# Seven products of a feed-forward tile tied in order on the tensor engine, and the second down weight of a tile made behind the sum that frees its accumulator

## The chip, the core and the metric

The kernel runs on one core of a Trainium2 chip. The metric is the device time of one execution in microseconds (us), the median of several executions. The kernel before takes 1226.12 us (three runs, 1225.51 to 1226.54). Besides these timed runs there is one profiled execution; every duration below comes from it.

The engines are named as in the profile: PE (tensor engine, matmuls), PEld (its weight loads), DVE (vector engine), ACT (scalar engine), POOL and SP (here they issue transfers). Each engine works through its own list of instructions in the order in which the program put them there.

## The reference

One decoder layer on 512 tokens of width 1024: a feed-forward, a mixer (attention and a recurrence, merged), and a second feed-forward. The change touches the two feed-forwards alone:

```python
def swiglu(x, w_gate, w_up, w_down):
    return (jax.nn.silu(x @ w_gate) * (x @ w_up)) @ w_down

f = swiglu(rms_norm(h, ffn1_norm_pre[l]), ffn1_w_gate[l], ffn1_w_up[l], ffn1_w_down[l])
h = h + 0.5 * rms_norm(f, ffn1_norm_post[l])
...
f = swiglu(rms_norm(h, ffn2_norm_pre[l]), ffn2_w_gate[l], ffn2_w_up[l], ffn2_w_down[l])
h = h + 0.5 * rms_norm(f, ffn2_norm_post[l])
```

The hidden width is 2816, that is 22 tiles of 128 columns. All inputs are float32.

## The kernel before, in words

**Numbers.** A float32 operand is split into a high part (a copy on ACT, rounded to the matmul's format) and a low part (source minus high part, on DVE); `split` does both, and its two instructions appear in the profile as L269 (ACT) and L270 (DVE). A product is three matmuls for each piece of the contraction: high by high, high by low, low by high.

**Feed-forward tiles.** `ffn` runs over the hidden tiles f = 0 to 21. The first n0 tiles (6 in the first feed-forward, 4 in the second) are plain. From f = n0 on a tile computes gate and up for all 512 tokens with seven products of half-size blocks in place of eight (a Strassen-Winograd scheme; the halves are of the contraction, of the tokens, and gate against up). `prod` issues them: p1, p5, p6, p2, p7, p3, p4, each twelve matmuls of 256 columns (lines 977 to 979). They accumulate in three places: `b` (bank 0 or 1, by turns from tile to tile) takes p1, p6, p7 and p4; `z` (bank 5) takes p5 and p3; `y` (bank 2) takes p2 on top of a copy of p1. Partial results are copied out on ACT between two products of one accumulator (L985 for c5 and c6, L998 for y), and added to later accumulator values on DVE (`sum_of`, L990). The sum of `b` and c5 after p7 must have read `b` before p4 may write it.

**Weights of a tile.** `w_forms_in_place` adds and splits a tile's weights one tile ahead (`prep`), with a priority that puts them ahead of the tile's own work. In the profile these are the rows w<-raw of L269 and L270, and the sums L623 to L627.

**Down projection.** Four hidden tiles at a time also go through a seven-product scheme. A `window` after a tile holds one to three of its products, run by `step` (matmuls of 512 columns, lines 891 to 893, two times six for each product). The windows are (p1, p2), (p5), (p6, p7), (p3, p4) in turn; in the first feed-forward the first eight tiles' products are caught up after f = 7 to 12, where two windows hold three products: (p1, p2, p5) after f = 7 and after f = 10. The weights of a step are made by `down_form`: a load by POOL into a buffer (`dr` or `npair`), a split into one of two buffers (`wd`, by turns), and then the issue of the load for the next product that uses the same source buffer (`supply`). The first two weights of a window (`due`) are made inside `prod`, between p2 and p7; the third is made inside the window behind its first step. Of all windows 24 have at least two weights and 6 have one.

**Order.** A scheduler puts the instructions of each engine in a list: at each point of its own model of time it takes the ready instruction of highest priority; priority is the order of the program, moved ahead by an offset where `tc.high_priority` says so (`AHEAD` = 100 for weights of the next tile, `EVAC` = 200 for copies and sums out of the accumulators). `tc.issue_after(ins)`, wrapped here as `behind(...)`, adds for each instruction of a block on the engine of `ins` that it comes behind `ins` in that engine's list; instructions of the block on other engines aren't touched. Before the change p1 of a tile is behind the last matmul before it, the steps likewise; the other six products are held by their data alone. In the kernel before, `down_form` for both weights stands in `behind("copy")`, behind the ACT copy c6.

Of the kernel before, what the change touches and what calls it, by code (L numbers as in the profile page):

```python
# [154 lines left out]
def hybrid_layer(ctx: ExitStack, tc: tile.TileContext, xT: bass.AP, xN: bass.AP, wst: bass.AP,  # L155
                 first: bass.AP, rows: bass.AP, wdn: bass.AP, wbig: bass.AP, consts: bass.AP, bias: bass.AP, out: bass.AP):
    nc = tc.nc
    DVE, ACT, PE = nc.vector, nc.scalar, nc.tensor
# [109 lines left out]
    def split(dh, dl, src):  # L268
        ACT.activation(dh, src, AF.Copy)  # L269
        DVE.tensor_sub(dl, src, dh.bitcast(F32))  # L270

    def acc_ps():
        turns["acc"] += 1
        return banks[(turns["acc"] - 1) % turns["n"]]
# [5 lines left out]
    def tmp(name):  # L280
        return tpool.tile([P, T], F32, name=name, tag="t")
# [503 lines left out]
    def ffn(n, x, r, forms_x, home, pss):  # L785
# [53 lines left out]
        def last_act(f):  # L839
            v = home.slot((f - LAST[0] - 1) % 8)  # L840
            return v[:, 0, :], v[:, 1, :]
# [12 lines left out]
        def supply(a, p):  # L854

            if p in ("p5", "p6", "p3"):
                dst, qs = home.x, {"p5": ("u0", "u1"), "p6": ("g0",), "p3": ("g1",)}[p]
            else:
                dst, qs = dr[p in ("p2", "p4")], {"p1": ("g0",), "p2": ("g1",), "p7": ("u0", "g0"), "p4": ("u1",)}[p]
            for i, q in enumerate(qs):  # L860
                load(dst, a, q, i > 0 or p in ("p6", "p3"))
            at[p] = dst
# [3 lines left out]
        def down_form(a, p):  # L866
            w = wdt[home.n % 2]
            home.n += 1
            split(w[:, 0, :], w[:, 1, :], at[p])
            ready[p] = w  # L870
            q = NEXT[p]
            a += p in ("p7", "p3", "p4")
            if a < SEVEN:
                supply(a, q)
# [78 lines left out]
        last = {}  # L953

        @contextmanager
        def behind(*engines):
            with ExitStack() as es:
                for e in engines:
                    if e in last:
                        es.enter_context(tc.issue_after(last[e]))  # L960
                yield

        def prod(f, w, due):

            g = tmp("g")
            b, y, z = b_of[f % 2][:, :HB], y_[:, :HB], z_[:, :HB]
            u = ub[:, f % 4, :] if 4 < f < LAST[0] else tmp("u")
            if n == 1 and f in (6, 8):
                u = tmp("u")

            def product(p, ps, start):
                if len(t[p][0].shape) == 4:
                    ps = ps.rearrange("q (b t) -> q b t", b=2)
                for k in range(4):
                    ks = slice(k * P, (k + 1) * P)
                    wh, wl, xh, xl = w[p][:, 0, ks], w[p][:, 1, ks], t[p][0][:, k], t[p][1][:, k]
                    PE.matmul(ps, wh, xh, start=start and k == 0, stop=False, skip_group_check=True)  # L977
                    PE.matmul(ps, wh, xl, start=False, stop=False, skip_group_check=True)  # L978
                    i = PE.matmul(ps, wl, xh, start=False, stop=k == 3, skip_group_check=True)  # L979
                last["PE"] = i.ins  # L980

            def copy(ps):
                c = tpool.tile([P, HB], F32, name="c", tag="c", bufs=CB)
                with tc.high_priority(offset=EVAC):
                    last["copy"] = ACT.activation(c, ps, AF.Copy).ins  # L985
                return c

            def sum_of(dst, ps, c):
                with tc.high_priority(offset=EVAC):
                    DVE.tensor_add(dst, ps, c)  # L990

            lead = f == n0
            with behind("PE"):
                product("p1", b, True)
            c1 = copy(b) if lead else None
            if not lead:
                with tc.high_priority(offset=EVAC):
                    ACT.activation(y, b, AF.Copy)  # L998
            product("p5", z, True)
            c5 = copy(z)  # L1000
            product("p6", b, False)
            c6 = copy(b)
            product("p2", y, lead)
            if lead:
                sum_of(g[:, lo_], y, c1)
            with behind("copy"):
                for a, p in due:
                    down_form(a, p)
            product("p7", b, False)
            sum_of(u[:, hi_], b, c5)  # L1010
            with tc.high_priority(offset=EVAC):
                ACT.activation(g[:, lo_], g[:, lo_] if lead else y, AF.Silu)
            product("p3", z, False)
            sum_of(g[:, hi_], z, c6)
            product("p4", b, False)
            last["ACT"] = ACT.activation(g[:, hi_], g[:, hi_], AF.Silu).ins
            with tc.high_priority(offset=EVAC):
                DVE.scalar_tensor_tensor(u[:, lo_], g[:, lo_], -1.0, b, op0=ALU.mult, op1=ALU.mult)
            last["DVE"] = DVE.scalar_tensor_tensor(u[:, hi_], g[:, hi_], -1.0, u[:, hi_], op0=ALU.mult,
                                                   op1=ALU.mult).ins  # L1020
            return u
# [41 lines left out]
        for at_, ev in enumerate(order):  # L1063
# [16 lines left out]
            elif ev[0] == "prep":  # L1080
                with behind("DVE", "ACT"):
                    forms[ev[1]] = w_forms_in_place(("gu", n, ev[1]))
            elif ev[0] == "prod":
                due = order[at_ + 1]
                u = prod(ev[1], forms.pop(ev[1]), [(due[1], p) for p in due[2][:2]] if due[0] == "window" else [])
                if ev[1] == 4:
                    part0(u)
            elif ev[0] == "finish":
                finish(ev[1], u)
            else:  # L1090
                for i, p in enumerate(ev[2]):
                    with behind("PE"):
                        step(ev[1], p)
                    if len(ev[2]) > 2 and i == 0:
                        down_form(ev[1], ev[2][2])
        with behind("ACT"):
            warm(eps)
        last = Act(*zip(*(last_act(f) for f in range(*LAST))))
# [295 lines left out]
    with ExitStack() as mx:  # L1394
# [127 lines left out]
        for hd in range(NH):  # L1522
# [9 lines left out]
            for kind, c in FILL[hd]:  # L1532
                if kind == "attn":
                    ws = fetch((kind, c))
                    for i in range(2):
                        ps = acc_ps()
                        gemm(ps, [w[:, i * T:(i + 1) * T] for w in ws], attn)
                        DVE.tensor_mul(facc[:, 2 * c + i, :], ps, facc[:, 2 * c + i, :])
                else:
                    ps = acc_ps()  # L1540
# [10 lines left out]
        for c in range(KC):  # L1551
            ps = acc_ps()
# [155 lines left out]
```

## Time and profile before

| | before |
|---|---|
| median of three runs | 1226.12 us (1225.51 to 1226.54) |
| the profiled execution, its own time | 1225.54 us |
| its span, first to last instruction | 1223.8 us |
| DVE busy | 974.9 us (80%) |
| ACT busy | 737.9 us (60%) |
| mean granted TensorE clock | 0.999 |
| matmuls of 256 columns, start to start when nothing is waited for | 0.12 us |
| the like of 512 columns | 0.23 us |

The profiled execution's time is 1.74 us more than its span, for what lies around the instructions, and 0.58 us below the median. A matmul's row gives a duration longer than the distance to the next one, since matmuls are pipelined; the distance between starts is what counts. An idle time in brackets at the end of a row is that of its engine just before, with the work that ended it.

### The profile page before, as it was taken

How to read it: one execution, taken by the hardware profiler on the slowest of the kernel's cores; microseconds unless marked ns; L12 is line 12 of the kernel's file. 1: busy time of each engine (PE TensorE's matmuls, PEld its weight loads, DVE VectorE, ACT ScalarE, POOL GpSimd, SP SyncE). 2: the span in 40 equal slices, each digit the busy share in tenths (PEclk: the TensorE clock that was granted, in tenths of full speed). 3: DMA queues.
4: the chain of work that ended last, by engine and by line, in shares of the span. 5: the costliest groups of instructions: out<-in, count | busy, mean ns of one | idle time of the engine just before them, and what ended most of it. 6: DMA issues, size and time to landing. Idle time of an engine off the chain costs nothing.

```text
span 1223.8 us, 19282 instructions
## 1 busy us (share of the span) xinstructions
PE 1211.8 (99%) x7664; PEld 1097.9 (90%) x7664; DVE 974.9 (80%) x1525; ACT 737.9 (60%) x1234; POOL 82.3 (7%) x135
## 2 busy tenths in 40 slices
PE   9999999999999999999999999999999999999997
PEld 8898989999878899999998888888899999999996
DVE  7998878988579887888766798755788887979864
ACT  7566665655556564656665787724556665656462
POOL 0001111100102000000000000000110010101000
PEclk9999999999999999999999999999999999999999
DMA  6336646464725222222234234324463555555441
GB/s 246 138 104 172 169 113 175 141 166 115 259 105 181 104 81 102 78 79 102 72 140 151 89 121 155 129 99 165 141 190 108 160 156 145 153 142 164 112 155 69
DMA packets 36986, 166.57 MB, mean 136 GB/s; under 512 B 4128, under 2 KB 7328, under 8 KB 24864
## 3 DMA queue, kind: packets, MB, share of 16 engines
q1 hardware_dynamic: 18288, 107.13, 24.8%
q0 software_dynamic: 18608, 58.20, 18.2%
q8 instruction: 60, 0.98, 0.3%
q14 instruction: 30, 0.25, 0.1%
HBM read 153.26 MB, written 7.86 MB: 132 GB/s over the span
## 4 chain that ended last, share of the span: by engine, by line
PE 94%; DVE 3%; ACT 1%; issue 1%; DMA 0%; DVEq 0%; ACTq 0%
PE bank L977 9%; PE bank L978 9%; PE bank L979 9%; PE bank L284 8%; PE bank L285 8%; PE bank L286 8%; PE bank L644 5%; PE bank L645 5%; PE bank L646 5%; PE bank L892 4%; PE bank L891 4%; PE bank L893 4%; PE bank L397 3%; PE bank L398 3%; PE bank L399 3%; DVE w L270 1%
## 5 line engine op out<-in xcount | busy, mean ns | idle before, releaser
L270 DVE TENSOR_TENSOR w<-raw,w 128x1024 fp32r<-128x1024 f32 (+1 forms) x272 | 297.5, 1103 | 68.4 <-ACT w L269 62.8
L269 ACT ACTIVATE w<-raw 128x1024 fp32r<-128x1024 f32 (+1 forms) x272 | 255.8, 960 | 96.3 <-PE bank L286 40.3
L977 PE MATMUL bank<-big,w 128*128 128x256 f32 x816 | 233.8, 287 | 3.0 <-DVE u L990 1.3
L978 PE MATMUL bank<-big,w 128*128 128x256 f32 x816 | 230.7, 283 | 0.0
L979 PE MATMUL bank<-big,w 128*128 128x256 f32 x816 | 229.4, 283 | 0.0
L977 PEld LDWEIGHTS bank<-big,w 128*128 128x128 f32 x816 | 156.2, 191 | 7.9 <-DVE u L990 2.0
L978 PEld LDWEIGHTS bank<-big,w 128*128 128x128 f32 x816 | 156.3, 192 | 1.6
L979 PEld LDWEIGHTS bank<-big,w 128*128 128x128 f32 x816 | 155.7, 192 | 0.0
L891 PE MATMUL bank<-wd,act 128*128 128x512 f32 x224 | 87.8, 392 | 0.0
L892 PE MATMUL bank<-wd,act 128*128 128x512 f32 x224 | 87.7, 392 | 0.0
L893 PE MATMUL bank<-wd,act 128*128 128x512 f32 x224 | 87.2, 389 | 0.0
L284 PE MATMUL bank<-big,w 128*128 128x512 f32 x176 | 68.5, 389 | 0.0
L285 PE MATMUL bank<-big,w 128*128 128x512 f32 x176 | 68.5, 389 | 0.0
L286 PE MATMUL bank<-big,w 128*128 128x512 f32 x176 | 68.5, 389 | 0.0
L644 PE MATMUL bank<-big,w 128*128 128x256 f32 x228 | 66.1, 290 | 0.0
L646 PE MATMUL bank<-big,w 128*128 128x256 f32 x228 | 64.8, 284 | 0.0
L285 PE MATMUL bank<-act,w 128*128 128x512 f32 (+1 forms) x184 | 64.7, 352 | 0.0
L286 PE MATMUL bank<-act,w 128*128 128x512 f32 (+1 forms) x184 | 64.7, 352 | 0.0
L284 PE MATMUL bank<-act,w 128*128 128x512 f32 (+1 forms) x184 | 64.6, 355 | 0.0
L645 PE MATMUL bank<-big,w 128*128 128x256 f32 x228 | 64.5, 283 | 0.0
L985 ACT ACTIVATE c<-bank 128x256 f32<-128x256 f32 x70 | 26.8, 383 | 61.0 <-PE bank L979 60.6
L270 DVE TENSOR_TENSOR wd<-npair,wd 128x1024 fp32r<-128x1024 f32 x24 | 29.4, 1224 | 39.2 <-ACT wd L269 39.2
(393 smaller groups left out, 3148.5 us busy)
## 6 DMA issues: line engine op xcount, KB each, us to landing
raw<-in_w SPq DMA_DIRECT2D x90, 1024.0 KB, 4.8
dr<-in_wdn POOLq DMA_DIRECT2D x40, 512.0 KB, 5.7
npair<-in_wdn POOLq DMA_DIRECT2D x32, 512.0 KB, 5.5
big<-act POOLq DMA_DIRECT2D x6, 512.0 KB, 3.3
h<-in_x SPq DMA_DIRECT2D x8, 256.0 KB, 5.1
h<-in_xn POOLq DMA_DIRECT2D x4, 512.0 KB, 5.2
raw<-in_wbig SPq DMA_DIRECT2D x2, 1024.0 KB, 4.7
kept_m<-h POOLq DMA_DIRECT2D x4, 512.0 KB, 2.9
```

The lines of the kernel that those rows point to most:

```text
L269: ACT.activation(dh, src, AF.Copy)
L270: DVE.tensor_sub(dl, src, dh.bitcast(F32))
L284: PE.matmul(ps, wh, xh, start=first, stop=False)
L285: PE.matmul(ps, wh, xl, start=False, stop=False)
L286: PE.matmul(ps, wl, xh, start=False, stop=last)
L644: PE.matmul(ps, wh, xh, start=start and k == 0, stop=False, skip_group_check=True)
L891: PE.matmul(ps, xh, wh, start=start and k == 0, stop=False, skip_group_check=True)
L892: PE.matmul(ps, xh, wl, start=False, stop=False, skip_group_check=True)
L893: i = PE.matmul(ps, xl, wh, start=False, stop=k == 1, skip_group_check=True)
L977: PE.matmul(ps, wh, xh, start=start and k == 0, stop=False, skip_group_check=True)
L978: PE.matmul(ps, wh, xl, start=False, stop=False, skip_group_check=True)
L979: i = PE.matmul(ps, wl, xh, start=False, stop=k == 3, skip_group_check=True)
```

## The change

Each of the seven products is now put in `behind("PE")`: on PE it comes behind the last matmul traced before it, so that the order is p1, p5, p6, p2, p7, p3, p4, then the steps of the window, then the next tile. The first weight of a window is still made behind the copy c6. The second (`due[1:]`) is traced behind the sum that follows p7, in `behind("sum")`; that sum is a DVE instruction, so that the DVE half of the split comes behind it on DVE. The ACT half of the split and the load that follows are in the block too, but on other engines.

```diff
             def sum_of(dst, ps, c):
                 with tc.high_priority(offset=EVAC):
-                    DVE.tensor_add(dst, ps, c)
+                    last["sum"] = DVE.tensor_add(dst, ps, c).ins
...
-            product("p5", z, True)
+            with behind("PE"):
+                product("p5", z, True)
             c5 = copy(z)
-            product("p6", b, False)
+            with behind("PE"):
+                product("p6", b, False)
             c6 = copy(b)
-            product("p2", y, lead)
+            with behind("PE"):
+                product("p2", y, lead)
             if lead:
                 sum_of(g[:, lo_], y, c1)
             with behind("copy"):
-                for a, p in due:
+                for a, p in due[:1]:
                     down_form(a, p)
-            product("p7", b, False)
+            with behind("PE"):
+                product("p7", b, False)
             sum_of(u[:, hi_], b, c5)
+            with behind("sum"):
+                for a, p in due[1:]:
+                    down_form(a, p)
             with tc.high_priority(offset=EVAC):
                 ACT.activation(g[:, lo_], g[:, lo_] if lead else y, AF.Silu)
-            product("p3", z, False)
+            with behind("PE"):
+                product("p3", z, False)
             sum_of(g[:, hi_], z, c6)
-            product("p4", b, False)
+            with behind("PE"):
+                product("p4", b, False)
```

## The prediction

> **What bounds the kernel now.** I read the page first, then the idle time of the tensor engine (PE) along its timeline, then the vector engine (DVE) and scalar engine (ACT) around each of its waits.
>
> ```profile
> span 1223.8 us, 19282 instructions
> PE 1211.8 (99%) x7664; PEld 1097.9 (90%) x7664; DVE 974.9 (80%) x1525; ACT 737.9 (60%) x1234; POOL 82.3 (7%) x135
> ```
>
> PE is busy for all but 12 us, so the change can win only what the feed-forwards lose in waits, and can lose whatever new waits it makes. The windows below are stages of PE work: the first three hold the places where the order on PE departs from the program's, the last is an undisturbed tile.
>
> ```profile
> 98.03:113.00 14.97, 13.58 (x98) 12.49 (x97) 12.52 (x19) 8.76 (x14) 2.28 (x3) 1.00 0.54 108
> 149.75:164.84 15.09, 14.97 (x108) 13.80 (x107) 9.33 (x13) 9.15 (x15) 1.71 (x2) 1.00 0.44 87
> 164.84:180.11 15.27, 14.75 (x99) 13.31 (x98) 14.38 (x23) 8.98 (x16) 1.10 (x2) 1.00 0.52 143
> 963.08:978.70 15.62, 15.62 (x110) 14.62 (x108) 13.51 (x20) 11.34 (x20) 1.43 (x2) 1.00 0.53 155
> ```
>
> The columns are the stretch, its length, and the busy time of PE, PEld, DVE, ACT and POOL, then the granted clock, DMA share and GB/s. The last stretch is one tile (84 matmuls of 256 columns) and two steps (24 of 512 columns): 15.62 us, PE never idle. With a step of twelve at 0.228 (2.74 us), the contents of the others without a wait would be: the first, one step and a tile, 15.62 - 2.74 = 12.88, so it loses 2.09; the second, the same and 11 products' matmuls of the next tile's p5 at 0.12, 14.20, loses 0.89; the third, two steps and a tile less those 11, 14.30, loses 0.97. Together 3.95 us, most of what the two feed-forwards lose at all, and the ceiling of a gain.
>
> **Tying the products.** It adds no instruction. In nearly all tiles PE already runs p1, p5, p6, p2, p7, p3, p4, so that the tie changes nothing there. The departures follow the two windows with three down products.
>
> ```profile
> 98.03 0.39 PE L891 MATMUL bank<-wd,act 128*128 128x512 f32 x1
> 98.26 0.28 PE L977 MATMUL bank<-big,w 128*128 128x256 f32 x1
> ...
> 100.56 0.38 PE L977 MATMUL bank<-big,w 128*128 128x256 f32 x1 [0.47 <-ACT c L985]
> ...
> 101.26 0.40 PE L892 MATMUL bank<-wd,act 128*128 128x512 f32 x1
> ...
> 96.36 1.05 ACT L269 ACTIVATE wd<-npair 128x1024 fp32r<-128x1024 f32 x1
> ...
> 99.51 1.22 DVE L270 TENSOR_TENSOR wd<-npair,wd 128x1024 fp32r<-128x1024 f32 x1
> ...
> 151.26 1.22 DVE L270 TENSOR_TENSOR wd<-npair,wd 128x1024 fp32r<-128x1024 f32 x1
> ```
>
> The third product's weight is made inside the window. Its first matmul (L891, at 98.03) needs the high part alone; the second (L892) needs the low part, which DVE finishes at 99.51 + 1.22 = 100.73. In between PE does p5 of the next tile and five matmuls of p3. Tied, it has nothing to do there: from 98.26 to 100.78 (a release takes 0.05, by the sum and the matmul of the chain below) it waits 2.52 us. The second such window starts at 149.75, its low part is there at 152.48: from 149.98 to 152.53, 2.55 us. What was late next goes: the wait of p3 for the copy c5 (0.47 idle at 100.56) and its like in the two later stretches, because p6 and p2 again lie between p5 and p3. So the 3.95 us of the three stretches become 5.07: **+1.12 us**. Bounds: DVE could take this split as soon as ACT is done (96.36 + 1.05 = 97.41), since only sums stand before it; then it ends at 98.63 and each wait is some 0.4, a gain; or one more pass of 1.22 comes ahead of it, 3.74 each. I take the times of before, since nothing ahead of these two splits on DVE waits for PE's later order.
>
> The clock in these stretches is granted at 1.00, and the longest distance between two starts there, 110.26 to 111.46, leaves it so. The Trainium skill (TensorE: Matmul & The Clock Gate, Part 1: The HAM clock gate) says that a window of about 3.4 us without work halves PE's clock until it has been busy as long; by it 2.5 us stay free of charge and 3.74 would not, which no run here shows.
>
> **The second down weight.** Per tile with two weights it moves one ACT copy (1.05), one DVE subtraction (1.22) and the loads that follow, 24 times. On DVE the subtraction leaves its place ahead of the sum. In one tile that place costs PE a wait:
>
> ```profile
> 109.85 1.22 DVE wd L270
> 111.07 0.35 DVE u L990
> 111.41 0.04 issue
> 111.46 0.39 PE bank L977
> ```
>
> The chain of waits shows p4 at 111.46 released by the sum, which stood behind the second weight; p3's last matmul was at 110.26, so 1.08 us, already in the 2.09 above. In the others the sum is just in time:
>
> ```profile
> 968.95 1.22 DVE L270 TENSOR_TENSOR wd<-npair,wd 128x1024 fp32r<-128x1024 f32 x1 [1.76 <-ACT wd L269]
> 970.10 1.22 DVE L270 TENSOR_TENSOR wd<-dr,wd 128x1024 fp32r<-128x1024 f32 x1
> 971.23 0.42 DVE L990 TENSOR_TENSOR ub<-bank,c 128x256 f32<-128x256 f32 x1
> ...
> 971.59 0.28 PE L979 MATMUL bank<-big,w 128*128 128x256 f32 x1
> 971.71 0.38 PE L977 MATMUL bank<-big,w 128*128 128x256 f32 x1
> ...
> 964.77 0.37 ACT L998 ACTIVATE bank<-bank 128x256 f32<-128x256 f32 x1 [0.60 <-PE bank L979]
> 966.15 0.39 ACT L985 ACTIVATE c<-bank 128x256 f32<-128x256 f32 x1 [1.01 <-PE bank L979]
> ...
> 968.82 1.05 ACT L269 ACTIVATE wd<-dr 128x1024 fp32r<-128x1024 f32 x1
> ...
> 970.03 2.01 ACT L269 ACTIVATE w<-raw 128x1024 fp32r<-128x1024 f32 x2
> ```
>
> What will DVE do in the freed 1.22? The tie holds DVE alone: ACT's half of the split loses its place behind c6. Its source and its buffer are ready early in the tile, and ACT idles there (0.60 ahead of 964.77, 1.01 ahead of 966.15), so the scheduler will put it there. It can push the copy at 964.77 by at most 0.45, to an end of 965.59, which its reader, two products later, doesn't feel. Then ACT has nothing between the first weight's copy and the copy of the next tile's weights (now at 970.03), and is in the state of a tile with one weight:
>
> ```profile
> 955.74 1.22 DVE L270 TENSOR_TENSOR wd<-npair,wd 128x1024 fp32r<-128x1024 f32 x1 [2.31 <-ACT wd L269]
> 957.18 1.23 DVE L270 TENSOR_TENSOR w<-raw,w 128x1024 fp32r<-128x1024 f32 x1 [0.22 <-ACT w L269]
> 958.32 0.42 DVE L990 TENSOR_TENSOR ub<-bank,c 128x256 f32<-128x256 f32 x1
> ...
> 956.10 1.05 ACT L269 ACTIVATE w<-raw 128x1024 fp32r<-128x1024 f32 x1
> ...
> 958.38 0.28 PE L979 MATMUL bank<-big,w 128*128 128x256 f32 x1
> 958.79 0.38 PE L977 MATMUL bank<-big,w 128*128 128x256 f32 x1
> ```
>
> There the next tile's weight (w<-raw) is ready a moment before p7 is done, DVE starts its 1.23 at 957.18, and the sum ends later than in the tile with two: p4 follows p3 after 0.41 in place of 0.12. That is **0.29 us** a tile. It decides the case: the sum that the change moves forward finds another subtraction in front of it, which starts 0.2 later than the one taken away.
>
> How many tiles: of the 24, six have the second weight behind the sum already. Twelve with f below 16 do not; among them are the two that follow the three-product windows. Six more (f = 17, 19, 20 in both feed-forwards) are like the one-weight tile f = 18:
>
> ```profile
> 126.62 0.42 DVE L990 TENSOR_TENSOR ub<-bank,c 128x256 f32<-128x256 f32 x1
> ...
> 1091.40 0.42 DVE L990 TENSOR_TENSOR ub<-bank,c 128x256 f32<-128x256 f32 x1
> ...
> 269.92 0.28 PE L979 MATMUL bank<-big,w 128*128 128x256 f32 x1
> 270.07 0.39 PE L977 MATMUL bank<-big,w 128*128 128x256 f32 x1
> ```
>
> The first two rows are the sums of the first and the last of ten tiles like the one at 963 (the other two are the following ones of the three-product windows); the last two show f = 18, where p4 loses 270.07 - 269.92 - 0.12 = 0.03. So 12 x 0.29 = 3.48 and 6 x 0.03 = 0.18: **+3.66 us**. Bounds: 0, if DVE takes the sum first, to 18 x 0.29 = 5.2. I take the value of the one-weight tiles, the nearest rows.
>
> Behind the sum the second subtraction falls in the gap before p4's end, as in the six tiles that have it there:
>
> ```profile
> 1049.86 1.22 DVE L270 TENSOR_TENSOR wd<-dr,wd 128x1024 fp32r<-128x1024 f32 x1
> ...
> 1051.86 0.39 PE L892 MATMUL bank<-wd,act 128*128 128x512 f32 x1
> ```
>
> It ends at 1051.08 and its first reader starts at 1051.86: 0.78 to spare, covered by the first step. If one more pass of 1.22 comes between, PE waits 0.44. The load behind it:
>
> ```profile
> dr<-in_wdn POOLq DMA_DIRECT2D x40, 512.0 KB, 5.7
> ```
>
> POOL issues it when the subtraction is through, so some 2 to 3 us later; 5.7 to land still leaves it ready before the next tile's down weights are made behind c6, about 13 us on. Later loads on POOL's queue wait for their own subtractions anyway. I cost it at nothing; a load that ACT reached too early would hold the copies behind it on ACT, below 1 us in the few tiles where the same buffer is needed at once.
>
> **Sum.** 1.12 + 3.66 = +4.78 us. The profiled execution's own time, 1225.54 (1.74 around its span), becomes 1230.3; it lay 0.58 below the median of 1226.12, so the median becomes **1230.9**.
>
> **The rivals.**
>
> *Sum first.* DVE takes the sum as soon as p7 is done, ahead of the next tile's weight; no 0.29 anywhere, and the two long waits remain: +1.12, **1227.2**. For it: in the tiles with two weights DVE is free 0.2 us before the sum is ready and the priority of a sum is higher; against it: all six one-weight tiles have the subtraction first, and it is ready first.
>
> *Faster.* The scheduler, which sees PE idle in the three-product windows, or an ACT relieved by earlier copies, brings their splits to DVE once ACT is done: two waits of 0.4, no other: 0.8 for 3.95, -3.15, **1223.0**. It decides if the splits start before 98.0 and 149.6. Against it: the sums ahead of them are next-tile work with a higher priority.
>
> *Second weight late.* With the next tile's subtractions first, the second weight slips by one more pass: 18 x 0.44 = 7.9 more, **1238.8**. For it: 0.78 is all there is; against it: six tiles hold it.
>
> *Long waits longer.* One more pass of 1.22 in each of the two, 2.4 more: **1233.3**. By the page on the clock gate, half the clock for some 3.4 us would add an estimated 1.7 to each.
>
> *Nothing done.* PE's order is the program's already and the order on DVE settles as before: 1226.1. Against it: the rows between 98.26 and 101.26.
>
> **How the numbers follow.** Forecast 0.47, sum first 0.17, faster 0.16, second weight late 0.12, longer waits 0.04, nothing done 0.04. The likeliest's own range is 1228.5 to 1233.5. The whole range reaches from the faster case to beyond the longer waits: 1222.8 to 1236; the late weight is left out. Faster by over 0.2% (2.45 us, about what a measurement tells from no change): 0.16; within it, sum first and nothing done, 0.21; slower 0.63.
>
> **What would show it.** Right: no L977 row between rows of L891 to L893; PE idle about 2.5 us inside each three-product window, ended by DVE wd L270; in the tiles with two weights DVE's order wd, w, sum, with p4 some 0.4 after p3's last matmul; ACT's copy of the second weight ahead of c6. Wrong: the sum right behind the first wd (then 1227.2); the 2.5 us shorter, or PE waits of L892 in ordinary windows.

## The result, and the profile after

The changed kernel takes 1257.36 us (median of six runs, 1253.26 to 1259.87) against 1226.21 before: a ratio of 1.0248, 95% interval 1.0238 to 1.0259. The forecast was 1230.9, with a range to 1236. The direction was right, the size wrong by 26 us. Of the executions behind the numbers below one, of the kernel without ties and with the subtraction alone moved, took 1472.84 us at a granted clock of 0.753; it enters no ratio.

From the page of the kernel after, its span, the busy times, the chain of waits by engine, and the median landing time of one kind of load; its profiled execution took 1259.35 us:

```profile
span 1257.6 us, 19277 instructions
PE 1226.1 (98%) x7664; PEld 1107.7 (88%) x7664; DVE 977.2 (78%) x1525; ACT 742.0 (59%) x1234; POOL 82.4 (7%) x135
...
PE 83%; DVE 7%; DMA 4%; issue 3%; ACT 2%; POOL 1%; DVEq 0%; ACTq 0%; POOLq 0%
...
dr<-in_wdn POOLq DMA_DIRECT2D x40, 512.0 KB, 6.7
```

The span grew by 33.8 us (1257.6 - 1223.8). Two things are to be seen. PE has the same 7664 matmuls, but is busy for 14.3 us more: the same work ran slower somewhere. And the chain now runs through transfers (DMA 4%) and POOL; the load dr<-in_wdn lands in 6.7 us, 5.7 before. The view of waits (engine and line, what it waited for, total us, times, longest) names the place. Before, and then after:

```profile
PE bank L977 <- ACT bank L998: 0.3, 1, 0.3
```

```profile
PE bank L977 <- ACT bank L998: 17.8, 7, 3.9
...
ACT wd L269 <- DMA dr<-in_wdn: 22.8, 6, 5.0
```

L998 is ACT's copy of p1 from `b` to `y`, and p6, which overwrites `b`, can't start before it has read `b`. PE's wait for it grew by 17.5 us. The second row says why ACT is late: six times its copy of a down weight waits for that weight's load. Before there is no such row. The timeline of one of the six places, after, sorted by engine (start, duration, engine, line, in brackets the idle time before and what ended it):

```profile
1003.41 1.23 DVE L270 TENSOR_TENSOR wd<-npair,wd 128x1024 fp32r<-128x1024 f32 x1 [1.69 <-ACT wd L269]
1006.00 0.42 DVE L990 TENSOR_TENSOR ub<-bank,c 128x256 f32<-128x256 f32 x1
1007.80 1.22 DVE L270 TENSOR_TENSOR wd<-dr,wd 128x1024 fp32r<-128x1024 f32 x1
...
1005.00 0.54 POOL L850 DMA_DIRECT2D npair<-in_wdn  x1 [10.94 <-DVE wd L270]
1009.21 0.87 POOL L848 DMA_DIRECT2D npair<-in_wdn  x1 [3.67 <-DMA npair<-in_wdn]
1009.78 0.84 POOL L850 DMA_DIRECT2D dr<-in_wdn  x1
...
1017.64 1.06 ACT L269 ACTIVATE wd<-dr 128x1024 fp32r<-128x1024 f32 x1 [3.08 <-DMA dr<-in_wdn]
1018.60 0.37 ACT L998 ACTIVATE bank<-bank 128x256 f32<-128x256 f32 x1
...
1016.22 0.28 PE L979 MATMUL bank<-big,w 128*128 128x256 f32 x1
1019.02 0.39 PE L977 MATMUL bank<-tx,w 128*128 128x256 f32 x1 [2.52 <-ACT bank L998]
```

The same tile and the next one before the change, likewise:

```profile
985.71 1.22 DVE L270 TENSOR_TENSOR wd<-dr,wd 128x1024 fp32r<-128x1024 f32 x1
986.85 0.42 DVE L990 TENSOR_TENSOR ub<-bank,c 128x256 f32<-128x256 f32 x1
...
987.29 0.54 POOL L850 DMA_DIRECT2D dr<-in_wdn  x1 [0.53 <-DVE ub L990]
990.28 0.88 POOL L848 DMA_DIRECT2D npair<-in_wdn  x1 [2.45 <-DMA npair<-in_wdn]
...
996.01 0.37 ACT L998 ACTIVATE bank<-bank 128x256 f32<-128x256 f32 x1 [0.60 <-PE bank L979]
998.83 0.38 ACT L985 ACTIVATE c<-bank 128x256 f32<-128x256 f32 x1 [1.06 <-PE bank L979]
999.11 2.00 ACT L269 ACTIVATE wd<-dr 128x1024 fp32r<-128x1024 f32 x2
```

This is a window of p3 and p4; p4's split frees the buffer `dr`, and its load fetches the weight of p2 for the very next window. Two ends moved towards each other:

- The load starts later. Measured from the start of the tile's sum (L990), POOL issued it after 0.44 us before (987.29 - 986.85) and after 3.78 now (1009.78 - 1006.00). Nearly all of that is the subtraction, which stood ahead of the sum and now ends at 1009.02. POOL adds its own part: its list has the two loads of p5's weight ahead, and the second, which adds onto the first, waits 3.67 us for the first to land; p2's load goes out 0.76 us after its buffer is free (1009.78 - 1009.02).
- It is wanted sooner. Before, ACT's copy stood behind c6 and came to its turn at 999.11, 11.8 us after the issue. Now it stands in ACT's list ahead of L998; ACT reaches it at 1014.56 (1017.64 - 3.08), 4.8 us after the issue. The load needs 7.8.

ACT executes its list in order, so L998 waits with the weight, and p6 behind L998. The other five places are the tiles whose second weight is p2's as well; start to start, less 0.12 for the matmul, the six waits are 2.4, 2.9, 3.8, 2.7, 4.1 and 2.6 us.

The second part of the loss stands in the windows of time (stretch, its length, busy time of PE, PEld, DVE, ACT and POOL, granted clock, DMA share, GB/s). After:

```profile
99.12:102.53 3.41, 1.55 (x6) 0.96 (x6) 3.39 (x5) 0.41 (x1) 0.52 (x1) 1.00 0.97 246
102.53:105.95 3.42, 3.42 (x11) 2.73 (x10) 2.65 (x5) 1.00 (x2) 0.35 (x1) 0.50 0.73 139
...
1078.74:1082.16 3.42, 1.60 (x14) 1.40 (x12) 1.96 (x4) 0.00 (x0) 0.00 (x0) 1.00 0.78 231
1082.16:1085.57 3.41, 1.31 (x11) 1.31 (x12) 0.00 (x0) 1.63 (x3) 0.00 (x0) 1.00 0.00 1
1085.57:1088.98 3.41, 3.41 (x19) 3.41 (x18) 1.23 (x1) 1.55 (x3) 0.00 (x0) 0.50 0.00 0
...
1013.89:1017.30 3.41, 2.61 (x22) 2.40 (x21) 1.51 (x3) 0.67 (x2) 0.00 (x0) 1.00 0.68 213
1017.30:1020.72 3.42, 1.70 (x14) 1.70 (x15) 0.00 (x0) 1.63 (x3) 0.00 (x0) 1.00 0.02 5
...
1150.42:1153.83 3.41, 3.41 (x18) 3.41 (x17) 0.96 (x1) 1.33 (x2) 0.00 (x0) 0.50 0.00 0
```

In seven stretches of 3.41 us, the first at 102.53 and the last at 1150.42, PE's granted clock is 0.50. Six of them lie behind five of the six waits, the first behind a three-product window. They hold 23.2 us of PE work, which would take half of that at full clock: by this estimate 11.6 us are lost. So the span's 33.8 are 17.5 of waits for L998, 11.6 of half clock, and 4.7 of all else. That this is near the 4.78 that the forecast held for the whole is not a test of its terms; they are looked at below.

### The profile page after: what moved, and what is told of

It reads as the page before. It is cut to its first block, busy times and chain, and to the rows that moved or that the text cites. A ratio compares the mean times of both kernels' runs of the same rounds, so it can differ in the third digit from the quotient of the medians.

```text
span 1257.6 us, 19277 instructions
## 1 busy us (share of the span) xinstructions
PE 1226.1 (98%) x7664; PEld 1107.7 (88%) x7664; DVE 977.2 (78%) x1525; ACT 742.0 (59%) x1234; POOL 82.4 (7%) x135
## 4 chain that ended last, share of the span: by engine, by line
PE 83%; DVE 7%; DMA 4%; issue 3%; ACT 2%; POOL 1%; DVEq 0%; ACTq 0%; POOLq 0%
PE bank L284 8%; PE bank L285 8%; PE bank L286 8%; PE bank L977 7%; PE bank L978 7%; PE bank L979 7%; PE bank L644 5%; PE bank L645 5%; PE bank L646 5%; DMA dr<-in_wdn 4%; PE bank L398 3%; PE bank L399 3%; PE bank L397 3%; PE bank L892 3%; PE bank L893 3%
## 5 line engine op out<-in xcount | busy, mean ns | idle before, releaser
L977 PE MATMUL bank<-big,w 128*128 128x256 f32 x816 | 236.4, 290 | 2.3 <-DVE u L990 0.4
L978 PE MATMUL bank<-big,w 128*128 128x256 f32 x816 | 233.6, 286 | 0.0
L979 PE MATMUL bank<-big,w 128*128 128x256 f32 x816 | 233.2, 286 | 0.0
L977 PEld LDWEIGHTS bank<-big,w 128*128 128x128 f32 x816 | 159.3, 195 | 7.6 <-DVE ub L990 4.7
L978 PEld LDWEIGHTS bank<-big,w 128*128 128x128 f32 x816 | 159.0, 195 | 1.3
L979 PEld LDWEIGHTS bank<-big,w 128*128 128x128 f32 x816 | 158.9, 195 | 0.0
L892 PE MATMUL bank<-wd,act 128*128 128x512 f32 x224 | 88.4, 395 | 1.8 <-DVE wd L270 1.8
L893 PE MATMUL bank<-wd,act 128*128 128x512 f32 x224 | 88.0, 393 | 0.0
L270 DVE TENSOR_TENSOR wd<-dr,wd 128x1024 fp32r<-128x1024 f32 x32 | 39.0, 1219 | 39.3 <-ACT wd L269 39.3
L644 PE MATMUL bank<-big,w 128*128 128x256 f32 x228 | 66.0, 290 | 0.0
L646 PE MATMUL bank<-big,w 128*128 128x256 f32 x228 | 64.7, 284 | 0.0
L645 PE MATMUL bank<-big,w 128*128 128x256 f32 x228 | 64.5, 283 | 0.0
```

The source lines that it names most:

```text
L892: PE.matmul(ps, xh, wl, start=False, stop=False, skip_group_check=True)
```

## The experiments

**The two parts apart.** First the ties alone, with both weights left behind c6; then the second weight alone, without ties:

```diff
-            product("p5", z, True)
+            with behind("PE"):
+                product("p5", z, True)
...
             with behind("copy"):
                 for a, p in due:
                     down_form(a, p)
```

> The seven products tied as in the change; both down weights behind the copy c6 as before. Theory (the scalar engine runs into a load that is not there): the six waits of 2.4 to 4.1 us are not there, since the scalar copy of the second weight keeps its place; the two three-product windows cost about 3.4 us of waits and 1.7 of half clock for the 3.95 they lost before, so 1227 to 1229 us, six waits of p6 absent. Rival (the ties leave the tensor engine without work to fill its waits): most of the 31 us is here, 1245 or more.

```diff
             product("p5", z, True)
...
             with behind("copy"):
-                for a, p in due:
+                for a, p in due[:1]:
                     down_form(a, p)
...
             sum_of(u[:, hi_], b, c5)
+            with behind("sum"):
+                for a, p in due[1:]:
+                    down_form(a, p)
```

> The second weight behind the sum as in the change; no ties. Theory: the six waits stay, because p5 and p3 can't fill them (the copy c5 is held on the scalar engine too), so 1248 to 1256 us with a lower granted clock. Rival (ties): about 1226 us.

The ties alone take 1227.56 us, ratio 1.0008 (0.9998 to 1.0018): no difference that can be told. The second weight alone takes 1258.03, ratio 1.0256 (1.024 to 1.0271), 2 us over the range expected. The whole loss is in the second part, and the ties neither make nor mend it. The waits of the second kernel show the same pair of rows as the full change:

```profile
PE bank L977 <- ACT bank L998: 21.0, 8, 4.5
...
ACT wd L269 <- DMA dr<-in_wdn: 25.1, 6, 5.5
```

**ACT's copy put back behind c6** in the changed kernel, the DVE half left behind the sum; once for all second weights, once for those of p2 alone:

```diff
             sum_of(u[:, hi_], b, c5)
-            with behind("sum"):
+            with behind("copy", "sum"):
                 for a, p in due[1:]:
```

> The change, with the scalar half of the second weight kept behind the copy c6 as before (behind copy and sum). Theory: no scalar copy waits for a load ahead of the copies that free the accumulators, the sum stands behind one subtraction: 1225 to 1229 us, clock 1.00. Rival (the move on the vector engine or the ties): 1240 or more.

```diff
             sum_of(u[:, hi_], b, c5)
-            with behind("sum"):
-                for a, p in due[1:]:
+            for a, p in due[1:]:
+                with behind("sum", *(["copy"] if p == "p2" else [])):
                     down_form(a, p)
```

> The change, with the scalar half kept behind c6 for p2's weight alone (the six tiles whose load comes from the window just before); the other second weights may go early as in the change. Theory: 1257.4 - 18.4 (six waits) - about 9 (half clock behind them) = 1230 us, the 0.3 us waits of p4 stay in the other tiles. Rival (all early copies cost alike): 18 of 24 tiles keep their cost, about 1250 us.

They take 1229.29 us, ratio 1.0021 (1.0011 to 1.003), and 1231.88 us, ratio 1.0043 (1.0028 to 1.0057); the first is 0.3 us over its range. One more tie on ACT, in the tiles where p2's weight is the second, takes back 25 of the 31 us (1257.36 - 1231.88 = 25.5). In the other tiles the early copy costs 2.6 us more (1231.88 - 1229.29): p4 loses 3.4 us there by the sum's later place on DVE, and nothing where all copies are kept. The second of these kernels is the change without its one fault, and lies 1.0 us from the forecast.

**No load to wait for.** The two kernels above move ACT's copy. They do not show whether that copy harms by its own 1.05 us, or by the load in front of it. So the copy stays early and the load goes:

```diff
             for i, q in enumerate(qs):
-                load(dst, a, q, i > 0 or p in ("p6", "p3"))
+                if p != "p2" or a == 0:
+                    load(dst, a, q, i > 0 or p in ("p6", "p3"))
             at[p] = dst
```

> The changed kernel, without the loads that p4's split issues for p2 (the first p2 keeps its load; the later ones split what lies in the buffer, so this part of the down weights is left out of the result). The instructions on PE, DVE and ACT and their order stay. Theory (ACT's early copy of p2's weight waits for a load that lands late, and holds the copies y and c that PE needs): the six waits of 2.4 to 4.1 us, 18.4 together, and the half clock behind them, some 8.8, go: 1230, between 1227 and 1233. Rival (the early copy delays ACT by its own 1.05 and DVE's new order does the rest, whatever the load does): the six waits stay, over 1250. Rival (the load is only half of it): 1236 to 1246.

1231.59 us, ratio 1.0035 (1.0022 to 1.0049). The longest waits of PE in the feed-forwards are now those of the three-product windows (one line is added, so that L892 is L893 here):

```profile
PE bank L893 <- DVE wd L270: 1.8, 2, 1.2
```

The row of waits for the copy of p1 is gone, and so is every stretch at half clock in the feed-forwards. The instructions on PE, DVE and ACT come in the same order in this trace as in that of the changed kernel. So the copy's early place by itself makes PE wait for no copy of p1; the load is what ACT, and behind it PE, waited for. The rival in which the six waits come of the copy's own 1.05 us falls.

**POOL's part of the lateness.** The load for p2 is issued by SP, so that it no longer stands behind the two loads of p5:

```diff
             else:
-                nc.gpsimd.dma_start(dst, stored(a, q))
+                (nc.sync if q == "g1" and dst is dr[1] else nc.gpsimd).dma_start(dst, stored(a, q))
```

> The changed kernel with the load for p2 issued by SP in place of POOL, so that it doesn't stand behind the two loads of p5 (the second of which waits for the first to land). Theory (the load is late above all since the subtraction that frees its buffer now follows the sum; POOL's list holds it some 0.8 us more): each of the six waits shortens by about 0.8, 5 in all, and perhaps a half-clock stretch or two go: 1248 to 1253. Rival (its place on POOL's list, and the transfers beside it, make the lateness): the waits fall under 1 us, 1230 to 1238. Rival (neither: SP's own list holds it as long): 1256 to 1260.

1248.14 us, ratio 1.0176 (1.0161 to 1.0191): 9 us back of the 31, not 25. From its waits and its list of transfers:

```profile
PE bank L977 <- ACT bank L998: 6.6, 2, 3.4
...
ACT wd L269 <- DMA dr<-in_wdn: 22.2, 7, 4.0
...
dr<-in_wdn SPq DMA_DIRECT2D x8, 512.0 KB, 8.3
```

Four of the six waits fell to 1.6 us or less, two stayed over 3. But ACT still waits 22.2 us for the load (22.8 in the changed kernel): the load is as late as it was. The four waits fell because the scheduler also changed ACT's order, among the six tiles in just those four. There the copy of p1, L998, now stands ahead of the weight's copy, and only c5 stands behind it:

```profile
195.16 0.37 ACT L998 ACTIVATE bank<-bank 128x256 f32<-128x256 f32 x1 [1.09 <-PE bank L979]
198.16 1.06 ACT L269 ACTIVATE wd<-dr 128x1024 fp32r<-128x1024 f32 x1 [2.63 <-DMA dr<-in_wdn]
```

In the two tiles where ACT's order stayed, the waits grew, from 2.4 to 3.6 us and from 2.7 to 3.3. At the place shown above SP issued the load at 1001.71, 3.05 us after the sum began (3.78 on POOL), but ACT could start its copy only at 1010.91, 9.2 later: what was won at the issue was lost in the transfer, which runs beside a load of 1024 KB for the next tile's weights and the loads of p5. So the time lies in the expected range by luck: the run does not show that POOL's list costs PE anything. How much of the lateness is the later subtraction and how much the transfers beside it was not separated.

**The move on its own, with ACT's copy kept.** In the kernel before, without ties, only the DVE half of the second weight goes behind the sum:

```diff
-                    DVE.tensor_add(dst, ps, c)
+                    last["sum"] = DVE.tensor_add(dst, ps, c).ins
...
             with behind("copy"):
-                for a, p in due:
+                for a, p in due[:1]:
                     down_form(a, p)
...
             sum_of(u[:, hi_], b, c5)
+            with behind("copy", "sum"):
+                for a, p in due[1:]:
+                    down_form(a, p)
```

> No ties on PE; the second weight's subtraction behind the sum, ACT's copy of it kept behind the copy c6. Theory: with ACT's copy in its old place the move of the subtraction costs what the run with both, 1229.3, has over the ties alone, 1227.6, so 1226.2 + 1.7 = 1227.9, between 1226 and 1229. Rival (the ties hide a loss of the later subtraction): over 1232. Rival (the move is a gain that the ties eat up): under 1225.

It took 1224.56 us, ratio 0.9979 (0.9969 to 0.9989): faster by 0.2%, and the theory (1226 to 1229) missed it. The rival in which the move is a gain that the ties eat up (under 1225) fits. The same kernel once more, for a trace:

> The same kernel as the run without ties and with the subtraction alone moved, for a trace of it. Theory (p4 of the tiles with two weights starts as soon as before, and the gain of 2.2 us comes from the tile behind a three-product window, where the sum stood behind that subtraction: 1.08 us each in two tiles): the time is again 1224 to 1225, and the first matmul of p4 follows p3's last after 0.12 to 0.5 us in those two tiles. Rival (the gain is spread over the other tiles): those two waits of about 1 us stay. Rival (no gain, a matter of the runs): 1226 to 1227.

1224.1 us, ratio 0.998 (0.997 to 0.9989). Its timeline in the tile that the forecast showed at 968.95, DVE and then the last matmul of p3 and the first of p4:

```profile
968.70 1.23 DVE L270 TENSOR_TENSOR wd<-npair,wd 128x1024 fp32r<-128x1024 f32 x1 [1.76 <-ACT wd L269]
970.22 0.42 DVE L990 TENSOR_TENSOR ub<-bank,c 128x256 f32<-128x256 f32 x1 [0.29 <-PE bank L979]
970.56 1.22 DVE L270 TENSOR_TENSOR wd<-dr,wd 128x1024 fp32r<-128x1024 f32 x1
...
971.70 0.28 PE L979 MATMUL bank<-big,w 128*128 128x256 f32 x1
971.82 0.28 PE L977 MATMUL bank<-big,w 128*128 128x256 f32 x1
```

Here DVE waits 0.29 us for p7 and takes the sum first, the order that the change meant to make. p4 follows p3 without a loss; before, the distance after its first matmul was 0.22 in place of 0.12 in sixteen such tiles, so the sum was 0.10 too late for it and not just in time (and the forecast's 3.95 us were not the ceiling of a gain). The 1.2 us that p4 lost at 110.26 are 0.4 here. Theory and rival each held a part: some 0.8 us come from that one tile and 0.1 from each of the sixteen, but in the tile behind the other three-product window p4, at 162.60, now loses 0.75 that it did not lose before. That makes 1.3 of the 2.2 us; the rest was not found.

With the ties the same move is a loss: 1229.29 us against 1227.56 of the ties alone. There, too, p4 loses nothing in the tiles with two weights; the loss lies in the windows of p6 and p7. A row of the kernel before with the one behind it, in such a window, and then the like place in the kernel with ties and ACT's copy kept:

```profile
1097.29 0.39 PE L893 MATMUL bank<-wd,act 128*128 128x512 f32 x1
1097.52 0.28 PE L977 MATMUL bank<-big,w 128*128 128x256 f32 x1
```

```profile
1101.02 0.50 PE L891 MATMUL bank<-wd,act 128*128 128x512 f32 x1 [0.24 <-DVE facc L910]
```

Without ties matmuls of the next tile slip in between the steps here, two before, six once the subtraction is moved, and PE has no wait. With ties a step waits for DVE's sum of a step before it (L910), which the later subtraction pushes back: start to start 0.4 to 0.5 us in each of the six windows, 2.6 in all, against 1.7 that p4 gains. So the ties took away what filled that wait.

**The three-product windows.** The forecast's rival of a gain was tried directly: the third weight of these windows gets the priority of the copies and sums. First in the kernel before, then with the ties:

```diff
                     if len(ev[2]) > 2 and i == 0:
-                        down_form(ev[1], ev[2][2])
+                        with tc.high_priority(offset=EVAC):
+                            down_form(ev[1], ev[2][2])
```

> The kernel before, with the third weight of the windows of three down products made ahead of what else stands on DVE. Theory (PE departs from the program's order there, and loses 3.95 us around it, because the low part of that weight is ready 2.5 us after its first matmul): the split ends some 2 us sooner, p5 of the next tile no longer slips in, and 2 to 3 us of the 3.95 come back: 1223 to 1225. Rival (what it is put ahead of is wanted as urgently): 1226 to 1229.

> The ties alone, with the third weight of those windows made ahead. Theory: of the waits of 2.3 us at the three-product windows 0.4 each stays, and no half clock follows them (1.7 each in the ties alone): 1227.6 - 2 x (1.9 + 1.7) is 1220.4 at the best; what the split pushes back costs some of it, so 1221 to 1225, below both kernels. Rival (the ties, not the late weight, make the loss): 1226 to 1228.

1222.63 us, ratio 0.9961 (0.9948 to 0.9973), and 1223.65 us, ratio 0.9973 (0.9963 to 0.9983). Both beat the kernel before and the changed one; the first won 4.1 us (1226.76 - 1222.63), more than the 2 to 3 expected. In the first, the split that began at 99.51 before begins at 97.68, right behind one sum of the step:

```profile
97.68 1.22 DVE L270 TENSOR_TENSOR wd<-npair,wd 128x1024 fp32r<-128x1024 f32 x1
```

With the ties PE still waits some 0.7 and 0.9 us in the two windows, and no stretch at half clock follows, as one does behind each of them in the ties alone.

The third weight ahead and the moved subtraction together, without ties:

> No ties; the second weight's subtraction behind the sum with ACT's copy of it kept behind the copy c6, and the third weight of the three-product windows made ahead. Theory (the two gains lie in different tiles and add: 4.1 by the third weight, 2.2 by the move): 1226.5 - 6.3 = 1220.2, between 1219 and 1222. Rival (both take the same wait, that of p4 in the tile behind a three-product window): no better than the third weight alone, 1222 to 1224.

1221.55 us, ratio 0.9968 (0.9956 to 0.998). That lies in the expected range, but it can't be told from the third weight alone either, so that the gains add is not shown. Its profiled execution was the slowest of its six (1226.22). In its trace PE waits 2.2 us for DVE (L806) at the first seven-product tile, with half clock behind, and 1.5 us for the sum at p4 (165.07) in the tile behind the second three-product window, where ACT waited 2.69 us for a down weight's load. The trace of the third weight alone has neither. Whether the other five executions have them stays open.

## Why the prediction was wrong

**The step that failed** is the cost of the load behind the moved split. The forecast put it "at nothing", since 5.7 us to land "still leaves it ready before the next tile's down weights are made behind c6, about 13 us on", and bounded a load that ACT reaches too early as "below 1 us in the few tiles where the same buffer is needed at once". Measured: 17.5 us of waits in six tiles, and behind five of them half clock, six stretches with an estimated 9.9 us lost. The cause is in the forecast's own text. Earlier in the same part it had moved ACT's copy from behind c6 to early in the tile; the load's cover was then computed with the copy in its old place. The right subtraction was ACT's new turn (4.8 us after the issue) against 7.8 to land: 3 us late. The bound of 1 us came from no row.

Two smaller errors in the same paragraph added to it. The landing time was the median of the page, while the places concerned take 7.1 to 8.5 us in the chain. And "Later loads on POOL's queue wait for their own subtractions anyway" left out that one of them adds onto an earlier load and waits for it to land, 3.67 us, and now stands ahead of p2's load on POOL. At the place shown that held the load by at most 0.76 us, and the run with the load on SP showed no gain from it.

**Ties, +1.12**: right in part in mechanism, in size partly by luck. The median of the ties alone is 1.2 us above the kernel before (1227.56 against 1226.35), but that can't be told from no change, and the profiled execution of it (1229.55, the slowest of ten) holds two stretches at half clock, which the forecast put at nothing. In the first three-product window after the change, a step's matmul of the other half slips in, and two waits stand in place of one:

```profile
98.87 0.39 PE L891 MATMUL bank<-wd,act 128*128 128x512 f32 x1
...
99.89 0.51 PE L891 MATMUL bank<-wd,act 128*128 128x512 f32 x1 [0.63 <-DVE facc L910]
101.62 0.50 PE L892 MATMUL bank<-wd,act 128*128 128x512 f32 x1 [1.23 <-DVE wd L270]
```

Start to start, less 0.23 each, that is 0.79 + 1.50 = 2.3 us for the 2.52 forecast. In the second such window of the ties alone it is 2.3 as well (2.55 forecast); in the changed kernel only 1.1. The forecast's "the tie changes nothing there" was wrong for the six windows of p6 and p7, where two matmuls of the next tile stood between the steps: in the changed kernel PE waits 0.3 us in four of them.

**Clock**: wrong. The forecast took waits of 2.5 us as free of charge. Behind the window just shown the clock fell to 0.50 for 3.41 us.

**Second weight, 0.29 in twelve tiles**: right. Over p4's first two matmuls, start to start, the 24 tiles lose 3.6 us more in the kernel without the load than with the ties alone, for 3.66 forecast; there eleven of the twelve show it. In the changed kernel nine do; of the other three, two stand behind a late load and one behind a three-product window. DVE and PE after, in the tile that stands for them:

```profile
988.93 1.23 DVE L270 TENSOR_TENSOR w<-raw,w 128x1024 fp32r<-128x1024 f32 x1 [0.22 <-ACT w L269]
990.07 0.42 DVE L990 TENSOR_TENSOR ub<-bank,c 128x256 f32<-128x256 f32 x1
...
990.12 0.28 PE L979 MATMUL bank<-big,w 128*128 128x256 f32 x1
990.54 0.39 PE L977 MATMUL bank<-big,w 128*128 128x256 f32 x1
```

The next tile's weight slips ahead of the sum, as forecast, and p4 follows p3 after 0.42. What makes this order is ACT's early copy, which frees ACT for the next weight: with the copy kept behind c6 the sum comes first, as in the rival "sum first", and the move is then a gain of 0.2% without ties. So the one fault, a block tied on DVE alone, cost both terms.

**ACT's early copy**: its place was foreseen. Where the load has landed it is as cheap as stated; in the tile of these rows it ran at 982.60, and c5 and c6 lost nothing.

**Rivals**: none of them named a load as late next. "Second weight late" came nearest in time (1238.8) with a mechanism that did not occur. What did occur, a load that ACT reaches too early, stood in the forecast as an aside under 1 us, and got no rival and no chance.

## What to carry to other kernels

When a step is moved by an order on one engine, look up where the scheduler will put its parts on the other engines, and compute the cover of every transfer it issues with the new places of both ends, the issue and the first reader. A copy moved early in a strictly ordered list is harmless only if its operand is there; otherwise everything behind it in that list inherits the wait, so tie it on that engine too. Work that slips into a wait is worth something: before an order is fixed, count where it does. A median landing time is no bound for a load that starts beside others.

## What the runs showed of the hardware

The granted clock fell behind waits shorter than expected. All half-clock stretches of the kernel after begin at whole multiples of 3.413 us from each other (143.49 - 102.53 = 12 times, 1150.42 - 1085.57 = 19 times), which fits a fixed grid; and in these traces it is the time that PE was busy in one stretch of that grid that goes with the clock of the next, not the length of one wait. In the rows above, stretches with 1.55 and 1.31 us of PE work in 3.41 were followed by half clock, those with 1.60, 1.70 and 2.61 were not: the wait of 2.7 us at 1016.22 was split between two stretches and cost no clock. Two other kernels bound the limit from nearer. The first pair of rows is of the ties alone, the second of the kernel with ACT's copy kept behind c6 for all second weights, both at the second three-product window:

```profile
152.49:155.91 3.42, 1.96 (x6) 1.21 (x7) 3.42 (x6) 0.70 (x2) 0.59 (x1) 1.00 0.85 170
155.91:159.32 3.41, 3.41 (x11) 2.74 (x11) 0.45 (x2) 1.52 (x3) 0.27 (x1) 0.50 0.76 102
```

```profile
152.77:156.18 3.41, 2.01 (x8) 1.40 (x8) 3.41 (x6) 0.60 (x1) 0.86 (x1) 1.00 0.95 252
156.18:159.60 3.42, 3.42 (x26) 3.21 (x26) 0.99 (x2) 2.08 (x4) 0.00 (x0) 1.00 0.96 165
```

Busy for 1.96 us, a stretch was followed by half clock; busy for 2.01, another was not. Six matmuls make up the 1.96, while fourteen made up the 1.60 that kept the clock: a matmul that stands alone counts longer in the busy time (0.50 us at 101.62) than one in a train (0.12 to 0.23 from start to start). So the limit, somewhere from 1.6 to 2.0, is not settled. The Trainium skill (TensorE: Matmul & The Clock Gate, Part 1: The HAM clock gate) says that the window of about 3.4 us runs freely; the traces agree. It also says that an idle window halves the clock; here a window in which PE worked for 1.55 us of 3.41 did. This also fits the spread of the changed kernel, 1253.26 to 1259.87 us, against 1221.47 to 1222.94 for the third weight alone, whose trace has no half clock in the feed-forwards. That the place on the grid makes the spread was not tried.
